# Rotary products and sums of q and k moved from POOL to DVE in a one-core decoder layer

## The chip, the core and the metric

The kernel runs on one core of a Trainium2 chip. Its engines are TensorE (PE; its weight loads are listed apart as PEld), VectorE (DVE), ScalarE (ACT), GpSimd (POOL) and SyncE (SP); SP's and POOL's queues issue the DMA transfers. The metric is the device time of one execution in microseconds, the median of several runs. The kernel before takes 1677.79 us (three runs, 1675.81 to 1681.36).

## The reference, cut to what matters

One step of a hybrid decoder layer in fp32, over 1024 prompt positions and 8 samples of 4 positions each, 1056 columns in all. Normed inputs are multiplied by one wide matrix; its columns feed sliding-window attention, a retention branch of four heads (key width 128, value width 256) and gates. The branches are merged, projected, and followed by a convolutional feed-forward part. The change touches the rotary embedding of the retention's q and k:

```
def rope_ret(x, pos):
    ang = 1.0 / (RET_THETA ** jnp.linspace(0.0, 1.0, DK_R // 2, dtype=jnp.float32))
    ang = jnp.repeat(ang, 2)
    th = pos.astype(jnp.float32)[:, None] * ang[None, :]
    cos = jnp.cos(th)[:, None, :]
    sin = jnp.sin(th)[:, None, :]
    x1 = x[..., ::2]
    x2 = x[..., 1::2]
    rot = jnp.stack([-x2, x1], axis=-1).reshape(x.shape)
    return x * cos + rot * sin
...
    qr = rope_ret(q_r.reshape(B, T, N_HEADS_R, DK_R).astype(jnp.float32), pos)
    kr = rope_ret(k_r.reshape(B, T, N_HEADS_R, DK_R).astype(jnp.float32), pos) * (DK_R ** -0.5)
```

## The kernel before, in words

Activations lie transposed, features on the 128 partitions and the 1056 columns along the row. Every fp32 operand of a large product is split into a high and a low part (ScalarE casts the high one, line 228 or 331; DVE subtracts, through the helper `ew`, whose DVE instruction has line 223 whatever it computes, and whose POOL instruction has line 225). A product is three matmuls, lines 255 to 257, into a PSUM bank of 264 columns.

The projections of the stage in question run as a generator, `stream`. It takes sixteen pairs of 128-column blocks of the weights, in the order q and k of the four retention heads first, then gates. Each pair is computed for two halves j of the columns, with seven products in place of eight: sums of weight blocks (tiles `s`, `w_raw`, made on DVE) are multiplied by sums of activations (tiles `xh`/`xl`, `ex`), and the results are added in three PSUM banks per half (`ps_q`). `in_split` loads a pair's two weight blocks (`w_raw`, 512 KB each, by SP, line 871) and makes the seven split operands (`w`, `w7x`). ScalarE copies banks into the SBUF tile `pair` (line 914); two DVE instructions (lines 937 and 939) add a further bank to parts of it. The seventh product goes into the bank that line 939 reads, so it has to wait for that instruction; it uses `w7x`, the last split of the pair. When a half is done, its follow-up is put on a list that `flush` empties one half later: for q and k `post_qk`, for gates others.

`post_qk` rotates the q block and the k block of a half, 128 x 528 each. `sh` gets the block with neighbouring partitions exchanged (DVE stream_shuffle, line 824), then the block is multiplied by the cosines (`rcos`), `sh` by the signed sines (`rsin`), and both are added. POOL's queue stores the two blocks to `qk_d` (line 830). There are 4 heads x 2 halves x 2 blocks, so 16 such blocks.

Between the steps of `stream` stands the retention of the samples, `sample(h)`: for each pair of samples it loads the 128 x 256 states (`s`), splits them (`s0s`), multiplies q and the states on TensorE (line 1050), multiplies keys and values (line 1055), updates the state on DVE (line 1056) and stores it by POOL's queue (line 1058). Later the prompt's retention runs between further steps of `stream`.

The source order is not the order on the engines: a planner, which estimates durations while the program is built, places each engine's instructions in one fixed sequence. On the chip each engine works through its sequence in order, and waits by semaphores for the others.

Of the kernel before, what the change touches and what calls it, by code (L numbers as in the profile page):

```python
# [47 lines left out]
def cols(tt):  # L48
    return slice(0, NS) if tt == SMP else slice(NS + P * tt, NS + P * tt + P)
# [71 lines left out]
def trunk(ctx, tc, I, O):  # L121
    nc = tc.nc
    mult, add, sub = ALU.mult, ALU.add, ALU.subtract
    V, S, G, TE = nc.vector, nc.scalar, nc.gpsimd, nc.tensor
# [60 lines left out]
    def pinned(ins):  # L185

        if PIN[0]:
            pin(ins)
# [31 lines left out]
    def ew(eng, out, in0, in1, op):  # L220

        if eng is V:
            pinned(V.scalar_tensor_tensor(out=out, in0=in0, scalar=1.0, in1=in1, op0=mult, op1=op))  # L223
        else:
            eng.tensor_tensor(out=out, in0=in0, in1=in1, op=op)
# [584 lines left out]
    def ST(name, shape, dt=F32, **kw):  # L810
        return rp.tile(list(shape), dt, name=name, **kw)

    def of_half(d, j):
        return d.rearrange("i p t -> p i t")[:, :, 2 * HW * j:2 * HW * (j + 1)]

    def both(t):
        return t.rearrange("p (i c) -> p i c", i=2)

    def post_qk(h):
        def post(j, o):  # L820
            c, d = (t[:, 2 * HW * j:2 * HW * (j + 1)] for t in (rcos, rsin))
            sh = [ST("sh", (P, 2 * HW), bufs=2) for _ in range(2)]
            for i in range(2):
                V.stream_shuffle(sh[i], both(o)[:, i], R_SHUF)
            for i in range(2):
                x = both(o)[:, i]
                ew(G, x, x, c, mult)
                ew(V, sh[i], sh[i], d, mult)
                ew(G, x, x, sh[i], add)
            st.dma_start(out=of_half(qk_d[h], j), in_=both(o))  # L830
        return lambda j, o: lambda: post(j, o)

# [493 lines left out]
    for tt in [0, 4, SMP, 1, 2, 3, 5, 6, 7]:  # L1326
# [3 lines left out]
        c = cols(tt)  # L1330
# [109 lines left out]
    for p in (A11, S1, A12, S4):  # L1440
        r, half = {A11: (0, 0), A12: (1, 0), S1: (0, 1), S4: (1, 1)}[p]
        for j in range(2):
            c = (2 * j + half) * HW
# [288 lines left out]
```

## Time and profile before

| what | value |
|---|---|
| median of three runs | 1677.79 us (1675.81 to 1681.36) |
| profiled execution, its own time | 1678.56 us |
| its span in the profile | 1676.8 us, TensorE's granted clock 0.998 |
| busy, share of the span | PE 97%, DVE 73%, ACT 51%, POOL 29% |
| stage of the shuffles (line 824) | 308.2 to 407.0 us |
| one shuffle of 128 x 528, median | 754 ns |
| POOL's product with the cosines, min / median / max | 1317 / 1634 / 2032 ns |
| POOL's sum, min / median / max | 1318 / 1644 / 2076 ns |

In the rows that follow, a group of instructions is given as line, engine, operation, what it writes and what it reads, shapes and count; then its busy time in us and the mean of one in ns, and behind the second bar the time its engine was idle just before, with what ended that idle time. In a timeline a row begins with its start and its duration in us, and an idle time before it stands in square brackets. In a table of stretches each engine has its busy time, with the number of instructions in brackets.

### The profile page before, as it was taken

The page shows a single profiled execution, that of the slowest core. Times are in us where ns is not written, and L with a number is a line of the kernel's source. Part 1 is how long each engine was busy: PE and PEld are TensorE (multiplying, and loading weights), DVE is VectorE, ACT ScalarE, POOL GpSimd, SP SyncE. Part 2 cuts the span into 40 slices and gives each one's busy share as a digit, 9 for nine tenths or more (in the row PEclk, how much of TensorE's full clock was granted, in tenths as well). Part 3 has the DMA queues.
Part 4 walks back from the last instruction along what each step waited for, and adds up shares of the span by engine and source line. Part 5 has one row for each costly group of instructions (what it writes and reads, how often), then busy time and mean ns, then how long its engine had stood idle before and what let it go on. Part 6 is the DMA issues. An engine that isn't in the chain of part 4 may idle for free.

```text
span 1676.8 us, 32469 instructions
## 1 busy us (share of the span) xinstructions
PE 1630.4 (97%) x12551; PEld 1587.5 (95%) x12551; DVE 1221.8 (73%) x2035; ACT 861.5 (51%) x1890; POOL 485.0 (29%) x686
## 2 busy tenths in 40 slices
PE   8999999899999999999999999999999999999997
PEld 7999989888999999999788999999999999999997
DVE  7887738699566566558757988888888888455476
ACT  6465634455655554554433655555555556443343
POOL 4242420465343433241412222212322223111102
PEclk9999999999999999999999999999999999999999
DMA  7212232445687786587623145444444448866664
GB/s 199 67 46 71 71 78 101 149 137 175 221 257 241 230 254 207 164 270 222 213 91 103 41 150 162 153 147 147 146 147 147 158 147 257 253 186 198 193 175 158
DMA packets 273291, 273.88 MB, mean 163 GB/s; under 512 B 23040, under 2 KB 234272, under 8 KB 273121
## 3 DMA queue, kind: packets, MB, share of 16 engines
q1 hardware_dynamic: 239377, 155.25, 31.9%
q0 software_dynamic: 33760, 116.57, 19.9%
q8 instruction: 98, 1.61, 0.4%
q14 instruction: 56, 0.46, 0.1%
HBM read 184.24 MB, written 87.49 MB: 162 GB/s over the span
## 4 chain that ended last, share of the span: by engine, by line
PE 64%; DMA 4%; DVE 4%; issue 3%; ACT 1%; POOL 1%; SPq 0%; DVEq 0%; POOLq 0%; ACTq 0%
PE ps_m L257 9%; PE ps_m L256 9%; PE ps_m L255 9%; PE ps_t L256 7%; PE ps_t L255 7%; PE ps_t L257 7%; PE ps_q L255 4%; PE ps_q L257 4%; PE ps_q L256 4%; DMA zt<-in_w_down 1%; DMA t<-z_d 1%; PE ps_b L1143 1%; PE ps_a L1147 1%; DVE xl L223 1%; PE ps_b L1145 1%
## 5 line engine op out<-in xcount | busy, mean ns | idle before, releaser
L255 PE MATMUL ps_q<-xh,w 128*128 128x264 f32 x512 | 152.2, 297 | 4.1 <-ACT pair L914 2.3
L223 DVE SCALAR_TENSOR_TENSOR w_lo<-w_raw,w_hi 128x1024 fp32r<-128x1024 f32 x83 | 103.3, 1250 | 64.2 <-ACT w_hi L228 57.4
L257 PE MATMUL ps_m<-xh,w_lo 128*128 128x264 f32 x512 | 145.8, 285 | 3.5 <-DVE w_lo L223 3.5
L255 PE MATMUL ps_t<-xh,w_hi 128*128 128x264 f32 (+2 forms) x524 | 148.9, 284 | 0.0
L256 PE MATMUL ps_t<-xl,w_hi 128*128 128x264 f32 (+2 forms) x524 | 148.7, 284 | 0.0
L257 PE MATMUL ps_t<-xh,w_lo 128*128 128x264 f32 (+2 forms) x524 | 148.1, 283 | 0.0
L255 PE MATMUL ps_m<-xh,w_hi 128*128 128x264 f32 x512 | 145.9, 285 | 0.0
L256 PE MATMUL ps_q<-xl,w 128*128 128x264 f32 x512 | 145.7, 285 | 0.0
L256 PE MATMUL ps_m<-xl,w_hi 128*128 128x264 f32 x512 | 145.4, 284 | 0.0
L257 PE MATMUL ps_q<-xh,w 128*128 128x264 f32 x512 | 145.0, 284 | 0.0
L223 DVE SCALAR_TENSOR_TENSOR w<-w_raw,w 128x512 fp32r<-128x512 f32 x152 | 110.4, 733 | 37.3 <-ACT w L331 36.0
L1482 DVE SCALAR_TENSOR_TENSOR c_out<-u_ext,fconst,c_out 128x1024 f32<-128x1024 f32 x96 | 121.9, 1280 | 2.6 <-ACT c_out L1478 0.5
L228 ACT CAST w_hi<-w_raw 128x1024 fp32r<-128x1024 f32 x62 | 65.3, 1053 | 100.9 <-PE ps_t L256 73.9
L331 ACT CAST w<-w_raw 128x512 fp32r<-128x512 f32 x152 | 93.6, 621 | 32.2 <-DVE w_raw L223 21.1
L255 PEld LDWEIGHTS ps_q<-xh,w 128*128 128x128 f32 x512 | 96.4, 188 | 5.9 <-ACT pair L914 2.8
L257 PEld LDWEIGHTS ps_m<-xh,w_lo 128*128 128x128 f32 x512 | 96.3, 188 | 4.3 <-DVE w_lo L223 4.3
L257 PEld LDWEIGHTS ps_t<-xh,w_lo 128*128 128x128 f32 x524 | 98.7, 188 | 0.0
L256 PEld LDWEIGHTS ps_t<-xl,w_hi 128*128 128x128 f32 x524 | 98.6, 188 | 0.0
L255 PEld LDWEIGHTS ps_t<-xh,w_hi 128*128 128x128 f32 x524 | 98.6, 188 | 0.0
L223 DVE SCALAR_TENSOR_TENSOR xl<-t,xh 128x1056 fp32r<-128x1056 f32 (+1 forms) x53 | 67.7, 1281 | 40.5 <-ACT xh L228 40.3
L256 PEld LDWEIGHTS ps_q<-xl,w 128*128 128x128 f32 x512 | 96.5, 188 | 0.5
L255 PEld LDWEIGHTS ps_m<-xh,w_hi 128*128 128x128 f32 x512 | 96.3, 188 | 0.1
(448 smaller groups left out, 6077.9 us busy)
## 6 DMA issues: line engine op xcount, KB each, us to landing
w_raw<-in_w_up SPq DMA_DIRECT2D x48, 512.0 KB, 4.2
w_raw<-in_w_in SPq DMA_DIRECT2D x42, 512.0 KB, 4.4
w_raw<-s_d SPq DMA_DIRECT2D x60, 256.0 KB, 3.9
t_d<-t POOLq DMA_DIRECT2D x24, 528.0 KB, 3.9
t<-t_d POOLq DMA_DIRECT2D x24, 528.0 KB, 5.2
t<-in_w_down SPq DMA_DIRECT2D x40, 256.0 KB, 4.6
s_d<-t POOLq DMA_DIRECT2D x20, 512.0 KB, 3.5
w_raw<-in_w_down SPq DMA_DIRECT2D x36, 256.0 KB, 5.3
```

The lines of the kernel that those rows point to most:

```text
L223: pinned(V.scalar_tensor_tensor(out=out, in0=in0, scalar=1.0, in1=in1, op0=mult, op1=op))
L228: pinned(S.copy(out=hi, in_=src))
L255: TE.matmul(ps, wh, xh, start=start, stop=False, **kw)
L256: TE.matmul(ps, wh, xl, start=False, stop=False, **kw)
L257: TE.matmul(ps, wl, xh, start=False, stop=stop, **kw)
L331: S.copy(out=t[:, 0:4], in_=src)
L1143: TE.matmul(po, sT, vt, start=True, stop=tt == 0)
L1145: TE.matmul(po, q, state["s"], start=False, stop=True)
L1147: TE.matmul(pk, kt, vt, start=True, stop=True)
L1482: V.scalar_tensor_tensor(out=c[:, NS:], in0=u[:, g, NU + t:NU + t + SEQ], scalar=sc[t], in1=c[:, NS:], op0=mult, op1=add)
```

## The change

The product with the cosines and the sum, both POOL tensor_tensor instructions before (line 225), become DVE instructions: `ew` makes a scalar_tensor_tensor with the scalar 1.0 of each (line 223). That is two instructions for each of the 16 blocks, 32 in all. Everything else in the source stays.

```diff
@@ post_qk @@
                 V.stream_shuffle(sh[i], both(o)[:, i], R_SHUF)
             for i in range(2):
                 x = both(o)[:, i]
-                ew(G, x, x, c, mult)
+                ew(V, x, x, c, mult)
                 ew(V, sh[i], sh[i], d, mult)
-                ew(G, x, x, sh[i], add)
+                ew(V, x, x, sh[i], add)
             st.dma_start(out=of_half(qk_d[h], j), in_=both(o))
```

The planner then orders the engines anew from here on; behind the retention's middle the sequences are the same again. Two places on DVE and one on POOL follow, with line numbers as in the profile; a line that begins with - stands only in the sequence before, one with + only in the changed one, and x2 means two alike in a row.

DVE, at the first rotation, from its first shuffle on (`ps_q_3686` is the bank that line 939 reads before the seventh product may go into it; `w_3717`, `w_3776` and `w_3812` are split operands of the next products):

```order
 L824 STREAM_SHUFFLE sh<-pair 128x528
+L223 SCALAR_TENSOR_TENSOR pair<-pair,rcos 128x528 x2
 L223 SCALAR_TENSOR_TENSOR sh<-sh,rsin 128x528 x2
 L223 SCALAR_TENSOR_TENSOR s0s<-s_3562,s0s 128x512
+L223 SCALAR_TENSOR_TENSOR pair<-pair,sh 128x528 x2
 L223 SCALAR_TENSOR_TENSOR w_3717<-s_3699,w_3717 128x512
 L1026 TENSOR_TENSOR v_3909<-vs_3904,v_3909 32x256
 L1027 TENSOR_TENSOR v_3909<-vs_3904,v_3909 32x256
-L223 SCALAR_TENSOR_TENSOR s_3699<-s_3699,w_raw 128x512
 L939 TENSOR_TENSOR pair<-ps_q_3686,pair 128x264
 L223 SCALAR_TENSOR_TENSOR w_3776<-w_raw,w_3776 128x512
 L223 SCALAR_TENSOR_TENSOR w_3812<-w_raw,w_3812 128x512
```

Four moved instructions stand ahead of line 939 there, and the weight sum s_3699, which stood ahead of it, comes later.

DVE, at the second rotation, about a half further (`ps_q_3818` is the bank of the next seventh product; `w_3970` is the first split operand of the following pair, `s_3969` its first weight sum, whose weights are just being loaded):

```order
 L1032 TENSOR_TENSOR t_3917<-ps_a,dm 128x128
+L223 SCALAR_TENSOR_TENSOR pair<-pair,sh 128x528 x2
+L223 SCALAR_TENSOR_TENSOR w_3970<-w_raw,w_3970 128x512
+L939 TENSOR_TENSOR pair<-ps_q_3818,pair 128x264
 L1036 TENSOR_TENSOR h_3920<-t_3917,h_3920 64x256
+L223 SCALAR_TENSOR_TENSOR s_3969<-w_raw 128x512
 L937 TENSOR_TENSOR pair<-ps_q_3817,pair 128x264
-L223 SCALAR_TENSOR_TENSOR s_3969<-w_raw 128x512
+L223 SCALAR_TENSOR_TENSOR w_raw<-w_raw 128x512
 L824 STREAM_SHUFFLE sh<-pair 128x528
-L223 SCALAR_TENSOR_TENSOR w_raw<-w_raw 128x512
-L939 TENSOR_TENSOR pair<-ps_q_3818,pair 128x264
```

Line 939 has moved ahead of the weight sum s_3969, and has a split of the following pair and two moved sums in front of it.

POOL, from the clearing of the samples' q tile on, in the changed kernel (the states' stores are line 1058):

```order
L976 MEMSET q_3559 128x576
L830 DMA qk_d<-pair 128x2x528 x2
L1058 DMA out_ret_sample<-s_3562 128x2x256
L1058 DMA out_ret_sample<-s_3564 128x2x256
L830 DMA qk_d<-pair 128x2x528
L1058 DMA out_ret_sample<-s_3974 128x2x256
L1058 DMA out_ret_sample<-s_4050 128x2x256
L830 DMA qk_d<-pair 128x2x528
```

Only stores are left here, and two of q and k come before the first state's; before the change a third block's product and sum also stood ahead of that state's store.

## The prediction

> **What bounds the kernel now.** First the head of the page and the busy times, then the stretches around the place of the change (it shuffles q and k from 308 to 407 us).
>
> ```profile
> span 1676.8 us, 32469 instructions
> PE 1630.4 (97%) x12551; PEld 1587.5 (95%) x12551; DVE 1221.8 (73%) x2035; ACT 861.5 (51%) x1890; POOL 485.0 (29%) x686
> ```
> ```profile
> core 0: us, PE busy (x) PEld busy (x) DVE busy (x) ACT busy (x) POOL busy (x), PEclk, DMA share, GB/s
> 300.00:342.00 42.00, 35.98 (x283) 34.72 (x284) 32.92 (x52) 17.65 (x46) 20.82 (x16) 1.00 0.49 158
> 342.00:412.00 70.00, 63.30 (x503) 60.93 (x503) 68.24 (x101) 36.81 (x103) 46.19 (x39) 1.00 0.52 160
> ...
> 425.00:720.00 295.00, 290.41 (x2242) 283.65 (x2241) 173.84 (x371) 158.23 (x389) 103.26 (x169) 1.00 0.72 230
> ```
> TensorE is the bound of the program: it lacks 46 us of the span. DVE's 73% is a mean over unlike stages. From 342 to 412 DVE is busy 68.24 of 70 us, more than TensorE (63.30): there DVE sets the pace. TensorE's idle time in the first two stretches is 6.0 and 6.7 us, and these 12.7 us are about all that a relief of DVE can return. After 425 us TensorE lacks 4.6 us in 295 and DVE has 121 us free.
>
> What TensorE waits for, from 300 to 425 us (us in total, times, longest):
>
> ```profile
> PE ps_b L1050 <- DVE s0s L223: 4.9, 7, 0.8
> PE ps_q L255 <- DVE pair L939: 3.4, 2, 1.7
> ...
> PE ps_q L255 <- DVE pair L937: 1.8, 2, 1.5
> ```
> 10.1 us of it end on DVE: seven short waits for the low half of a split state (s0s), four for a sum in a PSUM bank that is to be used again.
>
> **Removed from POOL.** Its groups from 295 to 430 us, then those of 342 to 412 alone:
>
> ```profile
> L225 POOL TENSOR_TENSOR pair<-pair,rcos 128x528 f32<-128x528 f32 x16 | 25.7, 1610 | 29.3 <-DVE sh L824 27.7 <-ACT w L331 1.5
> L225 POOL TENSOR_TENSOR pair<-pair,sh 128x528 f32<-128x528 f32 x16 | 25.4, 1592 | 7.7 <-DVE sh L223 7.4
> ```
> ```profile
> L225 POOL TENSOR_TENSOR pair<-pair,sh 128x528 f32<-128x528 f32 x11 | 17.7, 1612 | 5.4 <-DVE sh L223 5.2
> L225 POOL TENSOR_TENSOR pair<-pair,rcos 128x528 f32<-128x528 f32 x11 | 17.7, 1608 | 13.6 <-DVE sh L824 12.1 <-ACT w L331 1.5
> ```
> 51 us of work leave POOL, an engine with slack: by itself worth nothing. But these instructions lengthen DVE's. DVE's groups from 342 to 412 us:
>
> ```profile
> L223 DVE SCALAR_TENSOR_TENSOR sh<-sh,rsin 128x528 f32<-128x528 f32 x10 | 12.9, 1294 | 0.1
> L223 DVE SCALAR_TENSOR_TENSOR w<-w_raw,w 128x512 fp32r<-128x512 f32 x11 | 12.6, 1165 | 0.0
> L223 DVE SCALAR_TENSOR_TENSOR s0s<-s,s0s 128x512 fp32r<-128x512 f32 x10 | 9.2, 923 | 0.0
> ...
> L223 DVE SCALAR_TENSOR_TENSOR w<-s,w 128x512 fp32r<-128x512 f32 x5 | 5.1, 1021 | 0.0
> L1026 DVE TENSOR_TENSOR v<-vs,v 32x256 fp32r<-32x256 f32 x3 | 3.2, 1072 | 0.1
> ...
> L1027 DVE TENSOR_TENSOR v<-vs,v 32x256 fp32r<-32x256 f32 x2 | 0.8, 419 | 0.0
> ```
> The same shapes where POOL has no such products, from 425 to 720 us, and (the 528 wide one) from 740 to 1200:
>
> ```profile
> L223 DVE SCALAR_TENSOR_TENSOR w<-w_raw,w 128x512 fp32r<-128x512 f32 x42 | 28.3, 687 | 11.6 <-ACT w L331 11.6
> ```
> ```profile
> L223 DVE SCALAR_TENSOR_TENSOR t<-c_out 128x528 f32<-128x528 f32 x13 | 9.1, 698 | 0.0
> ```
> And one meeting of the two engines in the timeline (start, duration):
>
> ```profile
> 380.01 1.66 POOL L225 TENSOR_TENSOR pair<-pair,rcos 128x528 f32<-128x528 f32 x1 [0.32 <-DVE sh L824]
> ```
> ```profile
> 380.41 1.82 DVE L223 SCALAR_TENSOR_TENSOR sh<-sh,rsin 128x528 f32<-128x528 f32 x1
> ```
> POOL's product runs to 381.67; DVE's, begun inside it, ends 0.56 us after that, about its own 0.70 us: it stood until POOL was done. The lengthening in the stretch: sh 10 x (1294 - 698) = 6.0; w 11 x (1165 - 687) = 5.3; s0s 10 x (923 - 687) = 2.4; w from a sum 5 x (1021 - 687) = 1.7; L1026 against its twin L1027, 3 x (1072 - 419) = 2.0. Together 17.4 us, all of which I take as gone. The bounds: 0, if something else lengthens them, and 17.4.
>
> The Trainium skill says the same in "SBUF — State Buffer", section "Who interferes with whom": a DVE instruction with two SBUF inputs and a GpSimd instruction that reads SBUF exclude each other, and whichever starts second is blocked in full until the first ends. The trace agrees (1.82 us against 0.70). Its page "Perfetto Trace Analysis", section "Optimizing Scalar/DVE Operations", has a rule that speaks against this change: with a saturated DVE, offloading even to GPSIMD may make sense; it adds that between these two it might not help because of the shared port. By the first half alone the sum would be that of the second rival below.
>
> **Added to DVE.** A 528 wide scalar_tensor_tensor that is not held up, from its start to the next start, and one that follows the shuffle that it needs:
>
> ```profile
> 339.38 0.78 DVE L824 STREAM_SHUFFLE sh<-pair 128x528 f32<-128x528 f32 x1
> 340.20 0.71 DVE L223 SCALAR_TENSOR_TENSOR sh<-sh,rsin 128x528 f32<-128x528 f32 x1
> 340.82 0.68 DVE L1056 SCALAR_TENSOR_TENSOR s<-s,ps_a 128x512 f32<-128x512 f32 x1
> ```
> 0.62 us each (340.82 - 340.20). 22 of the 32 fall into 342 to 412: 13.6 us. One that stands right behind the shuffle it needs starts 0.82 us after that one's start (340.20 - 339.38), already more than its length of 0.78; the new order puts other work between in all places but one, so this is left out. DVE's work there becomes 68.2 - 17.4 + 13.6 = 64.4 us, against 63.3 of TensorE: a saving of 3.8. Two engines so close do not mesh without loss. The gain lies between 0 and the 6.7 us that TensorE lacks; I take the half, **3.4 us**, a little under DVE's own saving.
>
> **The first stretch, 300 to 342 us**, by its two long waits, each for L939. DVE's queue before the first:
>
> ```profile
> 309.45 0.77 DVE L824 STREAM_SHUFFLE sh<-pair 128x528 f32<-128x528 f32 x1
> 311.84 1.34 DVE L223 SCALAR_TENSOR_TENSOR sh<-sh,rsin 128x528 f32<-128x528 f32 x2 [1.62 <-DMA rsin<-in_rsin]
> 313.30 1.60 DVE L223 SCALAR_TENSOR_TENSOR s0s<-s,s0s 128x512 fp32r<-128x512 f32 x1
> 314.82 1.81 DVE L223 SCALAR_TENSOR_TENSOR w<-s,w 128x512 fp32r<-128x512 f32 x1
> ...
> 318.15 0.43 DVE L939 TENSOR_TENSOR pair<-ps_q,pair 128x264 f32<-128x264 f32 x1
> ```
> In the new order two cosine products follow the shuffles: 1.3 us inside the 1.62 us in which DVE waits for rsin anyway, so free; without that cover 1.3. The sines end at 313.2 as before, s0s at 313.9 (not 314.9), two sums at 315.2, w at 315.8, L1026 and L1027 (0.4 each) at 316.6, and the line's s sum now stands behind L939. L939 starts at 316.6, 1.5 us sooner, of a wait of 1.7.
>
> The second wait:
>
> ```profile
> 322.67 1.83 DVE L223 SCALAR_TENSOR_TENSOR w<-w_raw,w 128x512 fp32r<-128x512 f32 x1
> ...
> 331.84 0.69 DVE L223 SCALAR_TENSOR_TENSOR s<-w_raw 128x512 f32<-128x512 f32 x1 [1.54 <-DMA w_raw<-in_w_in]
> ...
> 333.68 0.43 DVE L939 TENSOR_TENSOR pair<-ps_q,pair 128x264 f32<-128x264 f32 x1
> ```
> ```profile
> 324.52 2.11 SPq L871 DMA_DIRECT2D w_raw<-in_w_in  x2
> ```
> L939 stood behind a sum that waited for weights, whose loads SP issued at 324.52, when the lengthened split ended (324.50), and by 326.6. In the new order L939 stands ahead of that sum and behind one split of the first load. With both splits unheld the loads go out no later, the first lands some 5.2 us on (331.84 - 326.6), near 330, and L939 runs near 331.5: 2 us sooner, so the 1.7 us wait goes. Together **3.2 us**; bounds 0 (the new order puts another wait there) and 6.0.
>
> **After 425 us** TensorE's, ScalarE's, POOL's and SP's orders still differ, to about 570 us, with the same work; the 4.6 us of idle time there may go either way. I take 0, bounds -2 and +2. POOL's queue keeps its stores: qk_d's store waits for a DVE sum instead of POOL's own, and stands ahead of the state's stores as before.
>
> **The sum.** The profiled execution took 1678.56 us, 1.8 around its span. 1678.56 - 3.4 - 3.2 = 1672.0. The median of the runs shown (1677.79) lies 0.8 below that execution, less than the runs differ among themselves, so 1672 stands for the changed kernel's median too.
>
> **The rivals.** (1) The waits only move, and the time stays: the ten s0s splits from 342 to 412 now have up to two moved instructions in front of them (1.24 us) instead of one lengthening (up to 1.0), 10 x 0.24 = 2.4 us back, and nothing is gained beside it in that stretch. 1678.56 - 3.2 + 2.4 = 1677.8 (1674.5 to 1679). For it: DVE's balance is only 3.8 us in 70. Against: in the first stretch the new order takes both long waits away.
> (2) Slower, DVE as the bound: moved instructions stand ahead of s0s and of L937 and L939, and the lengthening stays or is half of what I count. DVE would have 68.2 - 8.7 + 13.6 = 73.1 us of work in the 70, and with nothing gone 81.8: 3.1 to 11.8 us more, 1682 to 1690. It decides as soon as less than 11.8 of the 17.4 us goes (68.2 + 13.6 - 70). Against it: the same shapes take 687 and 698 ns elsewhere, and the meeting at 380 us.
> (3) All of TensorE's waits for DVE in both stretches go, 10.1 us: 1668.5, and at most the 12.7 us that it lacks there, 1665.9. For it: the long waits end on lengthened instructions. Against: TensorE and DVE stay within 3% of each other.
> (4) The change does not do what it says: the order lists show 32 DVE instructions more and no L225 left on POOL in this part, so 0.
>
> **Chances.** Forecast (1669 to 1674.5) 0.42, rival 1 0.34, rival 2 0.12, rival 3 0.12. About 0.3% (5 us) is what a measurement of this kernel tells from no change. Faster by more: most of the forecast and rival 3, 0.50; within: 0.37; slower: 0.13. The range 1666 to 1680 holds all but rival 2 and the far end of rival 3.
>
> **What would show it.** Right: sh, w and s0s near 690 ns from 300 to 412; DVE busy near 64 us for the work of 342 to 412; L939's two waits gone; TensorE's idle time from 300 to 425 near 7 us. Wrong: DVE full and s0s waits longer than 0.8 us; lengthening that stays with POOL quiet; new waits of TensorE after 425 us; or a stage that is no shorter though DVE has idle time.

## The result: slower by a third of a per cent, and the profile after

| kernel | median us | runs |
|---|---|---|
| before | 1675.92 | 20, 1672.02 to 1681.36 |
| changed | 1681.61 | 20, 1676.13 to 1688.19 |

The ratio of changed to before is 1.0036, 95% interval 1.0027 to 1.0045. Forecast were 1672 and a gain; it is a loss of 5.7 us. The profiled execution of the changed kernel took 1686.01 us, 4.4 more than its median.

The head of the page of the changed kernel, and its stretches (each engine's busy us and count of instructions, the granted clock, DMA):

```profile
span 1684.2 us, 32441 instructions
PE 1635.9 (97%) x12551; PEld 1592.9 (95%) x12551; DVE 1219.5 (72%) x2067; ACT 863.4 (51%) x1890; POOL 433.0 (26%) x654
```
```profile
core 0: us, PE busy (x) PEld busy (x) DVE busy (x) ACT busy (x) POOL busy (x), PEclk, DMA share, GB/s
300.00:342.00 42.00, 40.99 (x331) 40.45 (x332) 35.12 (x69) 20.63 (x53) 3.55 (x6) 1.00 0.50 165
342.00:412.00 70.00, 67.73 (x552) 66.68 (x551) 64.73 (x126) 39.24 (x100) 12.15 (x17) 1.00 0.49 153
412.00:425.00 13.00, 10.70 (x89) 10.49 (x88) 6.79 (x15) 6.93 (x19) 2.79 (x5) 1.00 0.83 266
425.00:500.00 75.00, 65.29 (x457) 60.67 (x458) 39.67 (x87) 38.52 (x99) 27.06 (x45) 0.95 0.68 220
500.00:570.00 70.00, 65.52 (x495) 64.02 (x494) 39.17 (x86) 39.28 (x91) 25.63 (x42) 0.98 0.67 215
```
The same stretches of the kernel before, which the prediction showed only in part:

```profile
412.00:425.00 13.00, 12.68 (x103) 12.25 (x102) 8.17 (x17) 10.06 (x25) 2.78 (x4) 1.00 0.43 145
425.00:500.00 75.00, 73.44 (x568) 71.41 (x567) 44.65 (x94) 41.73 (x104) 28.26 (x46) 1.00 0.80 255
500.00:570.00 70.00, 68.25 (x525) 66.55 (x524) 41.21 (x90) 40.41 (x98) 26.53 (x44) 1.00 0.69 219
```
From 300 to 412 us the change does what was forecast, and more: TensorE works 9.4 us more of these 112 us, with 97 matmuls more. From 412 to 570 us all of it is lost again, and more: 155 matmuls fewer (14, 111 and 30), 16.5 us of idle time instead of 3.6, and a clock of 0.95 and 0.98.

What TensorE waits for in the changed kernel, first from 300 to 425 us, then from 405 to 575 us (us in total, times, longest):

```profile
PE ps_q L255 <- ACT pair L914: 2.0, 2, 1.3
PE ps_a L1029 <- ACT r L1022: 1.7, 1, 1.7
...
PE ps_q L255 <- DVE pair L939: 0.2, 1, 0.2
```
```profile
PE ps_a L1130 <- DVE state L1150: 9.1, 5, 3.0
PE ps_q L255 <- DVE pair L937: 3.9, 2, 2.7
PE ps_q L255 <- ACT pair L914: 2.0, 1, 2.0
PE ps_b L1000 <- ACT o L994: 1.3, 1, 1.3
```
The waits for s0s and L939 are gone but for 0.2 us. In their place, 100 us later, stands L1150, in the retention of the prompt. That is a chain of 32 steps, one for each head and 128 positions: L1150 updates the state, which the next step needs, out of a PSUM bank `ps_a`, and L1130, a step's first matmul, writes into such a bank. There are two of them, so a step waits here for an earlier step's update ("the wait for the state" from here on). The kernel before has little of it in this window:

```profile
PE ps_a L1130 <- DVE state L1150: 1.7, 2, 1.1
```

The retention itself begins late: L1130 of the kernel before, then of the changed one (min, median and max duration, then the first and the last start).

```profile
L1130 PE MATMUL ps_a<-qk x64: 270/273/377, 448.8 to 674.8; 128*128 128x128 f32 x64
```
```profile
L1130 PE MATMUL ps_a<-qk x64: 269/275/567, 455.8 to 682.8; 128*128 128x128 f32 x64
```
7.0 us at its beginning and 8.0 at its end; the spans differ by 7.4. This although TensorE had done 83 matmuls more by 425 us (97 - 14). So TensorE had done other work instead: the matmuls of `stream`. Counted in TensorE's sequences as the planner left them, this many `ps_q` matmuls stand ahead of the last sample (its first product with v) and of steps of the retention:

| sequence of | sample 4 | step 1 | step 5 | step 7 | step 9 |
|---|---|---|---|---|---|
| kernel before | 808 | 1008 | 1100 | 1178 | 1274 |
| changed kernel | 951 | 1132 | 1226 | 1226 | 1226 |

The source says nothing of this. With 32 instructions more on DVE and as many fewer on POOL, the planner placed 143 matmuls more of `stream` ahead of the last sample; why it did was not looked into. Steps 5 to 10 of the retention then follow each other with no product of `stream` between them.

### The profile page after: what moved, and what is told of

It is laid out like the page before. It is cut to its first block, busy times and chain, and to the rows that moved or that the text cites. A ratio compares the mean times of both kernels' runs of the same rounds, so it can differ in the third digit from the quotient of the medians.

```text
span 1684.2 us, 32441 instructions
## 1 busy us (share of the span) xinstructions
PE 1635.9 (97%) x12551; PEld 1592.9 (95%) x12551; DVE 1219.5 (72%) x2067; ACT 863.4 (51%) x1890; POOL 433.0 (26%) x654
## 4 chain that ended last, share of the span: by engine, by line
PE 79%; DMA 8%; DVE 7%; issue 3%; ACT 2%; SPq 1%; POOL 0%; DVEq 0%; ACTq 0%; POOLq 0%
PE ps_m L256 9%; PE ps_m L257 9%; PE ps_m L255 9%; PE ps_t L256 7%; PE ps_t L257 7%; PE ps_t L255 7%; PE ps_q L255 4%; PE ps_q L257 4%; PE ps_q L256 4%; PE ps_mm L255 3%; PE ps_mm L256 3%; PE ps_mm L257 3%; DMA zt<-in_w_down 1%; DMA w_raw<-in_w_in 1%; DVE w_lo L223 1%
## 5 line engine op out<-in xcount | busy, mean ns | idle before, releaser
L223 DVE SCALAR_TENSOR_TENSOR w<-w_raw,w 128x512 fp32r<-128x512 f32 x152 | 103.5, 686 | 38.3 <-ACT w L331 38.1
L255 PEld LDWEIGHTS ps_q<-xh,w 128*128 128x128 f32 x512 | 97.5, 191 | 10.4 <-DVE pair L937 5.1
L257 PEld LDWEIGHTS ps_q<-xh,w 128*128 128x128 f32 x512 | 97.3, 191 | 0.2
```

The costliest lines, as they stand in the source:

```text
L255: TE.matmul(ps, wh, xh, start=start, stop=False, **kw)
L257: TE.matmul(ps, wl, xh, start=False, stop=stop, **kw)
```

## The experiments

Theory A: the move of the 32 instructions gives what was forecast for 300 to 425 us, and the planner's new sequences lose more than that. Theory B: the sequences are harmless, the work on DVE or the lack of it on POOL costs the time. All runs stood beside runs of the kernel before on the same chip, whose medians were 1675.9 to 1677.1 us.

**The two halves of the change apart.** A list of instruction numbers, chained engine by engine, gives each engine the sequence of the other kernel:

```diff
             trunk(ctx, tc, ins, outs)
+        hold_order(nc, tc)
```
First the move alone: products and sums on DVE around their sine product, and otherwise every engine in the sequence of the kernel before.

> The moved products and sums run on DVE as in the change, but every engine keeps the sequence of the kernel before: each cosine product stands on DVE right ahead of its block's sine product, each sum behind the next instruction but one after it; POOL only loses its 32. Kernel before 1675.9 us, changed kernel 1681.6 us. Theory A, the loss is the planner's new sequences behind 412 us: this kernel keeps the gain of 300 to 412 us (5 to 9 us) and loses nothing later, 1667 to 1671, with a granted clock of 0.997 or more. Theory B, the loss comes from the work on DVE itself, whatever the sequence: 1679 to 1683.

Measured: 1666.57 us, ratio 0.9948 (0.9930 to 0.9965). Second, the sequences alone: products and sums on POOL as before, every engine in the sequence of the changed kernel.

> The other half of the exchange: products and sums on POOL as before the change, every engine in the sequence of the changed kernel, POOL with the four instructions of a pair right ahead of the store of that pair. Theory A (the sequences cost): slower than the changed kernel, since the lengthened DVE instructions come back and the waits behind 412 us stay, 1685 to 1692. Theory B (the work on DVE costs): back to the kernel before, 1674 to 1678.

Measured: 1692.83 us, ratio 1.0096 (1.0077 to 1.0115). As parts of 1676 us:

| ratio to before | sequence of before | sequence of the changed kernel | what the sequence adds |
|---|---|---|---|
| on POOL | 1 | 1.0096 | +16.1 us |
| on DVE | 0.9948 | 1.0036 | +14.7 us |
| what the move adds | -8.7 us | -10.1 us | |

Within the intervals the two effects add up, and they have opposite signs. Theory B falls. The move in the old sequence, from 405 to 575 us and its L1130:

```profile
PE ps_b L1143 <- issue: 1.7, 1, 1.7
PE ps_a L1130 <- DVE state L1150: 1.0, 1, 1.0
PE ps_q L255 <- DVE pair L937: 0.9, 1, 0.9
```
```profile
L1130 PE MATMUL ps_a<-qk x64: 270/273/377, 441.7 to 665.8; 128*128 128x128 f32 x64
```
The retention begins 14.1 us earlier than in the changed kernel and hardly waits. From 425 to 570 us (the clock stands behind the five engines):

```profile
425.00:570.00 145.00, 142.38 (x1096) 138.99 (x1095) 84.36 (x185) 80.31 (x200) 56.03 (x94) 1.00 0.78 249
```
```profile
425.00:570.00 145.00, 130.82 (x950) 124.69 (x951) 78.84 (x172) 77.80 (x190) 52.69 (x86) 0.96 0.68 218
```
The first row is the move in the old sequence, the second the changed kernel: 146 matmuls, at 145 / 1096 = 0.132 us each 19.3 us. Idle time takes 11.6 of it (14.2 against 2.6). Nearly all of the rest is that matmuls take longer: 950 at 142.38 / 1096 would have been busy for 123.4 us, not 130.8, which is 7.4 less. The clock accounts for about 5 of these 7.4 us, as an estimate: 0.96 instead of 1.00 over 130.8 us is 5.2. Where the other 2 come from was not taken apart.

**Single waits of the changed kernel.** One load of weights was put ahead of the load of a state on SP's queue; in a second kernel the copies of the k and v caches by POOL's queue were issued at 723 us instead of 448. Both hold the changed kernel's sequence otherwise. (Exchanging the whole queues of SP or POOL between the two sequences was not tried.) In the two blocks that follow, the order of issue is given in words:

```diff
-SP: state load (L1010), weight load (L871)
+SP: weight load (L871), state load (L1010)
```
```diff
-POOL: copies to k_sample and v_sample, stores of the retention
+POOL: stores of the retention, copies to k_sample and v_sample
```


> The changed kernel in its own sequence, but one weight load (the one issued at 415.86 us) goes ahead of the state load on SP in front of it, which waited for a store to land until 415.39 us. If that queue is the cause of TensorE's wait of 2.66 us at 425 us and of the half clock behind it (0.83 from 425 to 435 us, about 1.7 us): the wait shrinks to under 1 us, the clock stays at 1.00 there, 1677.5 to 1680 against 1681.6. If another wait is right behind it: no change, 1681 to 1682.

> The changed kernel in its own sequence, but the two cache copies of POOL's queue (issued at 448 us) are issued behind the last gate store, near 718 us. If they slow the weight load of 449 us (12.7 us to land, others about 5): it lands in 5 to 7 us, TensorE's wait of 2.0 us at 462.8 us and the clock of 0.93 and 0.90 behind it go, and the waits for the retention's state at 484 and 492 us shrink: 1675 to 1679 against 1681.6. If the retention's own loads slow it: 1681 to 1682.

Measured: 1680.03 us (ratio 1.0027, 1.0013 to 1.0041) and 1681.29 us (1.0032, 1.0016 to 1.0048), both not to be told from the changed kernel. In the first the 2.7 us wait at 425 us shrinks to 1.2, in the second the wait at 463 us is gone; with the copies late TensorE waits for the state instead, from 405 to 575 us:

```profile
PE ps_a L1130 <- DVE state L1150: 10.1, 5, 3.5
```
So the loss hangs on neither of these two transfers.

**The place of the stream's products.** If theory A is right in its particulars, one rule is enough, and the planner may do the rest anew: the first matmul of each product, pinned, stays behind all that stands ahead of it in the program on TensorE.

```diff
+    HOLD = [0]
...
+                        first = TE.matmul(ps, t[:, k], xh, start=p in (A11, S1) and k == 0, stop=False, **kw)
+                        if HOLD[0] and (k == 0 or HOLD[0] == 2):
+                            pin(first)
...
     adv(18)
+    HOLD[0] = 1
     for h in range(4):
         for _ in sample(h):
             adv(3)
+    HOLD[0] = 0
```


> The changed kernel, planned anew, with one rule more: while the four samples are worked (behind adv(18), until the last of them) the first matmul of each of the stream's products must stay behind everything that stands ahead of it in the program on TensorE. The stream's products then stand 254, 434, 614 and 794 ahead of samples 1 to 4 (changed kernel: 281, 527, 800, 951) and 1008, 1064, 1100, 1178, 1274 ahead of the retention's steps 1, 3, 5, 7, 9, as in the kernel before (changed kernel: 1132, 1193, 1226, 1226, 1226). Theory A (what the change lost, it lost because the planner let the stream's products run ahead of the samples, so that the retention began late and then had no products left between its steps): 1667 us, 1664 to 1671; the first L1130 (its line as the kernel before numbers it) near 442 us instead of 455.8; waits of TensorE for the state, L1150, from 405 to 575 us below 4 us instead of 9.1. Theory B (it is the new sequence on DVE, ScalarE and the queues, not the products' place): 1678 to 1684, and waits for the state of 7 us or more.

Measured: 1668.87 us, ratio 0.9956 (0.9941 to 0.9971), the first L1130 at 442.9 us, and the waits for the state (here L1158, as lines have moved) 1.9 us. Its row from 425 to 570 us has 142 matmuls more than the changed kernel's, and full clock:

```profile
425.00:570.00 145.00, 141.63 (x1092) 138.18 (x1091) 84.27 (x185) 80.36 (x198) 56.46 (x94) 1.00 0.77 244
```
Theory A holds, and with the products put back the change is worth making: this kernel is faster than both. The rule lets the planner order the other engines anew as well, so it shows that the place of the products is enough to take the loss away, not that all else in the changed sequences is free. And it has a price: from 300 to 425 us TensorE now waits 5.5 us for h (0.3 before). The rule without the move, as a control:

> Kernel before, products and sums on POOL, planned anew with the rule that holds the stream's products behind the samples; samples then have 254, 434, 614, 794 products ahead of them (before: 254, 448, 628, 808), the retention's steps the same as before. Theory A (the rule only puts the place of the products back, the gain is that of the move): as the kernel before, 1676 us, 1673 to 1679. Rival (the rule gives a gain of its own, samples and retention that begin a little sooner): 1669 to 1672.

Measured: 1676.74 us, ratio 1.0002 (0.9992 to 1.0013). The rule gives nothing of its own.

The same rule kept up through the retention:

> As the one with the rule in the samples, but the rule goes on through the retention: its steps 1, 3, 5, 7, 9 then have 938, 986, 1082, 1178, 1274 of the stream's products ahead of them, 48 a step from the start. Theory A: there is nothing more to gain from step 7 on, where both have the same place, and the first steps come 60 to 80 products (some 8 us) sooner; the time is that of the other within 3 us, 1664 to 1671. Rival: at the retention's start its data (masks, states, r and z behind the samples' stores) are not there 8 us sooner, so TensorE waits there with its products held back behind the wait: 1672 to 1676.

Measured: 1688.40 us, ratio 1.0075 (1.0060 to 1.0090). Theory A's number falls, and the rival was right in kind and 12 us short in size. The retention now starts at 435.2 us, 7.7 us sooner than with the rule in the samples alone, but not all that its first step needs is there. From 405 to 575 us TensorE's largest waits are these:

```profile
PE ps_b L1150 <- DVE sT L1140: 5.6, 1, 5.6
PE ps_q L914 <- DVE pair L945: 3.3, 2, 2.7
PE ps_a L1137 <- DVE state L1157: 2.8, 2, 2.3
```
The first of them hangs on the load of the mask (`dm`), by which DVE makes sT; it was issued at 436.9 us and kept DVE until 444.3:

```profile
DVE sT L1140 <- DMA dm<-in_dmask: 7.1, 1, 7.1
```
Behind it the clock is low (from 440 to 450 us):

```profile
440.00:445.00 5.00, 0.33 (x1) 0.33 (x2) 0.49 (x2) 0.35 (x2) 1.26 (x2) 0.61 0.45 159
445.00:450.00 5.00, 5.00 (x26) 4.46 (x26) 1.12 (x2) 2.46 (x9) 1.14 (x2) 0.71 0.27 95
```
Step 7, with 1178 products of `stream` ahead of it in both kernels, starts at 482.1 us here and at 472.5 with the rule in the samples alone. So an early start is worth nothing where a step's data are not there yet, and equal counts alone do not make an equal time.

**One of the two operations.** The sums alone on DVE, then the products with the cosine alone, in the sequence of the kernel before:

```diff
-                ew(G, x, x, sh[i], add)
+                ew(V, x, x, sh[i], add)
```
```diff
-                ew(G, x, x, c, mult)
+                ew(V, x, x, c, mult)
```


> Kernel before with its own sequence on every engine held, and the sums alone on DVE, each right behind the sine product that it needs; POOL keeps the products with the cosine. Theory A (what the move gains is the lengthening of DVE's instructions beside POOL's; 17.4 us from 342 to 412 us for 22 products and sums, equally long on POOL): half of it goes, so half of the 9.6 us that both together gave: 1671.5 us, 1669 to 1674, and DVE's sh, w and s0s between 690 and their length before, 1294, 1165 and 923 ns. Rival (the gain is the handing to and fro between DVE and POOL, which one operation left on POOL keeps whole): within 2 us of the kernel before, 1674 to 1678.

> Kernel before with its own sequence on every engine held, and the products with the cosine alone on DVE, right behind the shuffle; POOL keeps the sums. Theory A: as for the sums alone, 1671.5 us, 1669 to 1674. Rival (the gain hangs on one of the two: the product with the cosine stands beside DVE's product with the sine in every pair, the sum beside whatever comes next): 1667 to 1669 here, and 1674 to 1676 for the sums alone.

Measured: sums alone 1676.48 us, ratio 1.0006 (0.9994 to 1.0018); products alone 1669.09 us, ratio 0.9961 (0.9946 to 0.9976). Not half and half: the products alone give 6.5 us, which the intervals do not tell from the 8.7 of both, and the sums alone nothing. (Each sum stands right behind its sine product here; another place was not tried.) DVE's groups from 342 to 412 us, of the sums alone and then of the products alone:

```profile
L223 DVE SCALAR_TENSOR_TENSOR sh<-sh,rsin 128x528 f32<-128x528 f32 x10 | 14.0, 1399 | 0.1
L223 DVE SCALAR_TENSOR_TENSOR pair<-pair,sh 128x528 f32<-128x528 f32 x11 | 7.8, 709 | 3.4 <-POOL pair L225 2.5
...
L223 DVE SCALAR_TENSOR_TENSOR s0s<-s,s0s 128x512 fp32r<-128x512 f32 x10 | 6.8, 682 | 0.0
```
```profile
L223 DVE SCALAR_TENSOR_TENSOR w<-w_raw,w 128x512 fp32r<-128x512 f32 x11 | 12.8, 1190 | 0.0
L223 DVE SCALAR_TENSOR_TENSOR s0s<-s,s0s 128x512 fp32r<-128x512 f32 x11 | 8.8, 801 | 0.0
...
L223 DVE SCALAR_TENSOR_TENSOR sh<-sh,rsin 128x528 f32<-128x528 f32 x10 | 7.0, 698 | 0.0
```
With the sums alone DVE's sine product still stands behind POOL's, and then the sum, and all that is queued behind it, waits for POOL's product as well (it ends 2.5 of the 3.4 us idle). With the products alone DVE waits for POOL nowhere in these groups, though w and s0s are still lengthened. TensorE's waits for s0s from 300 to 425 us are 6.4 us in the one and 3.0 in the other. Why short s0s splits come later in the one than long ones in the other was not taken apart further.

Last, the products alone, planned anew with no sequence held. The planner's sequence then lies between those of the two kernels:

> Only the products with the cosine on DVE, the sums on POOL, no sequence held: the planner then puts 260, 477, 674, 864 of the stream's products ahead of the samples and 1042, 1123, 1168, 1211, 1274 ahead of the retention's steps 1, 3, 5, 7, 9, between the kernel before (808 ahead of sample 4; 1008 and 1178 ahead of steps 1 and 7) and the changed one (951; 1132 and 1226). The same move in the sequence of the kernel before took 1669.1 us. Theory A: about 0.3 to 0.6 of the 15 us that the changed kernel's sequence costs come on top, 1674 to 1678. Rival (the products' place does harm only where five steps have none between them, as in the changed kernel): 1668 to 1672.

Measured: 1674.99 us, ratio 0.9990 (0.9977 to 1.0003): 4.9 us more than with the sequence held (0.9990 - 0.9961), as theory A had it. TensorE's waits for the state from 405 to 575 us are 4.3 us, between 1.7 (before) and 9.1 (changed).

| kernel | `ps_q` matmuls ahead of sample 4, step 1, step 7 | ratio | L1130 first, us |
|---|---|---|---|
| move, old sequence | 808, 1008, 1178 | 0.9948 | 441.7 |
| move, rule in the samples | 794, 1008, 1178 | 0.9956 | 442.9 |
| products alone, planned | 864, 1042, 1211 | 0.9990 | 450.2 |
| move, planned (the change) | 951, 1132, 1226 | 1.0036 | 455.8 |
| no move, the change's sequence | 951, 1132, 1226 | 1.0096 | 463.1 |
| move, rule to the end | 794, 938, 1178 | 1.0075 | 435.2 |

## Why the prediction was wrong, point by point

- **Lengthening goes: right.** DVE's groups of the changed kernel from 342 to 412 us:

```profile
L223 DVE SCALAR_TENSOR_TENSOR w<-w_raw,w 128x512 fp32r<-128x512 f32 x12 | 8.3, 688 | 1.1 <-ACT w L331 1.0
L223 DVE SCALAR_TENSOR_TENSOR pair<-pair,sh 128x528 f32<-128x528 f32 x11 | 7.6, 701 | 0.1
...
L223 DVE SCALAR_TENSOR_TENSOR sh<-sh,rsin 128x528 f32<-128x528 f32 x10 | 7.0, 702 | 0.0
...
L223 DVE SCALAR_TENSOR_TENSOR s0s<-s,s0s 128x512 fp32r<-128x512 f32 x9 | 6.2, 684 | 1.1 <-ACT s0s L228 1.1
```
w, sh and s0s are at 684 to 702 ns. The moved instructions take 0.70 each, and DVE is busy 64.73 us in the stretch, forecast 64.4. Rival 2 (lengthening that stays) falls.
- **The first two stretches: right.** Forecast were 3.4 and 3.2, together 6.6 us. The move alone gave 8.7 us, with an interval of 5.9 to 11.7, and by its own row TensorE is busy 118.16 us there, against 111.96 before (35.98 + 63.30 + 12.68), which is 6.2 more:

```profile
300.00:425.00 125.00, 118.16 (x942) 114.64 (x943) 108.89 (x210) 69.45 (x183) 20.56 (x29) 1.00 0.52 166
```
By stretches that is 1.9 us from 300 to 342 (3.2 forecast), 4.0 from 342 to 412 (3.4 forecast) and 0.3 behind them. The first is smaller because its term rested on the new place of L939, which the old sequence does not have: there TensorE still waits 2.5 us for L939. In the changed kernel its idle time from 300 to 425 us is 5.6 us (7 forecast) instead of 13.0. Rival 3's 10.1 us lies within the interval too.
- **L939's two waits: gone in the changed kernel,** 0.2 us of 3.4 left, and with them the s0s waits that rival 1 had growing.
- **"After 425 us ... I take 0, bounds -2 and +2": the step that failed.** It measured +14.7 us (ratio 1.0036 against 0.9948). The prediction saw that the sequences of TensorE, ScalarE, POOL and SP differ and that the work is the same, and took 4.6 us of idle time for what is at stake (it is that up to 720 us; up to 570 it is 3.3). Idle time bounds a gain, not a loss. What the runs showed in its place: the new sequence puts more products of `stream` ahead of the samples, so the retention begins 14.1 us later than with the move alone, has none of them left to fill the waits of its steps 5 to 10, and makes TensorE wait 9.1 us for the state instead of 1.0, with a clock of 0.96 instead of 1.00 from 425 to 570 us. That the place had moved could be told beforehand by counting the products in the two sequences (1178 against 1226 ahead of step 7, 1100 against 1226 ahead of step 5); the size could not. The sign "new waits of TensorE after 425 us" was the one that came.
- **The sum.** With the forecast's other terms and the measured one: 1672.0 + 14.7 = 1686.7, against the profiled 1686.0 and the median 1681.6. Its start was 2.6 us high, as the median of the 20 runs before is 1675.92 and not 1678.56. From that median, with the move's 8.7 and the 16.1 that the sequences cost with the work on POOL, it comes to 1675.9 - 8.7 + 16.1 = 1683.3. No rival had this mechanism; that rival 2's time (1682 to 1690) comes close is luck, as the lengthening that it needs went.

## What to carry to other kernels

Where a planner sets the sequence, a small edit is two changes: the work that it moves, and the sequences that come out new. Price the second by counting, at each point of a serial chain, how much independent work stands ahead of it and how much is left between its steps, look whether a step's data can be there when it starts, and hold that place by a rule in the source before judging the first. And where two engines hold each other up, try each operation alone before moving both: here the products alone gave 6.5 us and the sums alone nothing.

## What the hardware showed that was not expected

A short wait of TensorE cost more than its length. In the changed kernel (the clock stands behind the five engines' columns):

```profile
425.00:435.00 10.00, 9.64 (x65) 9.34 (x66) 5.64 (x11) 7.70 (x19) 1.86 (x3) 0.83 0.38 134
...
464.00:466.00 2.00, 2.00 (x7) 1.53 (x6) 2.00 (x5) 1.45 (x6) 0.37 (x1) 0.50 0.00 0
...
540.00:542.00 2.00, 0.00 (x0) 0.00 (x0) 0.68 (x3) 0.00 (x0) 0.00 (x0) 1.00 1.06 408
542.00:546.00 4.00, 3.87 (x19) 3.87 (x20) 3.16 (x9) 0.58 (x2) 0.79 (x1) 0.57 0.59 181
```
Three waits with their ends at 425.36 us (2.66 long), 462.77 (1.98) and 542.13 (2.98) each have a stretch at half clock behind them; two, at 484.35 (1.96) and 492.29 (2.28), have none. The trace's record of the granted clock has 0.50 for 3.41 us from 426.13, from 463.68 and from 542.18 us on, which is about 1.7 us lost each time, and these three times lie 11 and 23 times 3.41 us apart. With the first wait cut to 1.2 us by the earlier load, the clock from 425 to 435 us stayed at 1.00. The Trainium skill, "TensorE: Matmul & The Clock Gate", section "Part 1: The HAM clock gate (the "warmup" mystery)", puts the array back to half rate after an idle window of about 3.4 us and calls the window free-running. The free-running part agrees with the whole multiples of 3.41 us and with waits of like length that do and do not pay; here shorter waits, from 1.98 us on, were enough. How much idle time it takes was not measured.

It also fits the scatter: the changed kernel's 20 runs spread over 12 us and those that took longer show a lower mean clock, by and large (1676.3 us at 0.997, 1685.7 at 0.992): about 2 us for each 0.001.
